# One scan over 128 partitions for both directions of an S5 layer, with ScalarE turning the states back, in a two-layer encoder trunk

## The chip, the core and the metric

The kernel runs on one core of a Trainium2 chip. The metric is the device time of one execution in microseconds (us), taken as the median of three runs. Five engines work side by side, each through its own queue and in program order: TensorE (PE in the rows, with its weight loads as PEld), VectorE (DVE), ScalarE (ACT), GpSimd (POOL) and SyncE (SP), which here issues the large loads. They wait for each other through semaphores.

## What is computed

The program is a trunk of two layers over 512 tokens of 1024 channels in float32. Layer 0 has a convolution and attention mixer, layer 1 a bidirectional state-space (S5) mixer; each is followed by a mixture of 16 experts. The change lies in the S5 mixer alone, cut here to its core:

```python
def s5_scan(u, ...):              # u: (B, S, 64 groups, 16); 64 complex states per group
    bu_re = jnp.einsum('bsgc,gpc->bsgp', u, bb_re)      # and bu_im
    # h_t = lambda * h_{t-1} + bu_t, complex, over the 512 tokens
    _, _, h_re, h_im = lax.associative_scan(combine, (a_re, a_im, bu_re, bu_im), axis=1)
    return (jnp.einsum('bsgp,gcp->bsgc', h_re, c_re)
            - jnp.einsum('bsgp,gcp->bsgc', h_im, c_im))

def s5_mixer(h, ...):
    y_f = s5_scan(u, ...)                                       # forward
    y_b = jnp.flip(s5_scan(jnp.flip(u, axis=1), ...), axis=1)   # backward, other parameters
    z = jax.nn.gelu((y_f + y_b).reshape(B, S, D) + d_skip * hf)
    val, gate = jnp.split(z @ w_glu, 2, axis=-1)
    return val * jax.nn.sigmoid(gate)
```

## The kernel before

The program runs four phases after each other: mixer 0, experts 0, mixer 1 (S5), experts 1. In mixer 1 the 512 tokens are cut into 64 chunks of 8 tokens. A state is carried from chunk to chunk by a scan, and what happens within a chunk is done by matmuls with tables that were prepared earlier. The 64 groups are worked in 8 **octets** of 8 groups. Partitions 0 to 63 hold the 64 states of the forward direction, partitions 64 to 127 those of the backward one.

Since the multiplier of a state is complex and DVE scans real numbers, the phase is taken out first by a table `E` and put back afterwards; the scan itself multiplies by the magnitude `rho` alone. For each octet there are five steps:

- `inputs(o)`: 32 matmuls on TensorE (64 rows of the trace, each matmul shown as two) take the tokens `U` into PSUM tiles (`mm` or `po`), 64 columns of the stationary `W` per direction, with `U` streamed.
- `turn_in(o)`: two DVE products (L1271, `t<-mm` or `t<-po`) and two POOL sums (L1290, L1291) give the scan's input `XP`; ACT lays out the multipliers `RT` with zeros between the groups (L1293 for the forward half, L1294 for the backward one).
- `scan(o)`: DVE scans real and imaginary part, each in two instructions: the forward half by L1304 and the backward half, with its operands read and written from the last chunk to the first, by L1306. Two DVE products with `E` (L1271, `t<-gr`) and two POOL sums (L1312, L1313) then give the states `Hs`.
- `outputs(o)`: 24 matmuls (48 rows) on TensorE, with `U` and `Hs` as stationary operands, into an `ac` tile, and a gelu on ACT (L1331) into `ZY`.
- `turn_z(q)`, for every second octet: eight transposes, and for each piece a copy on ACT (L1343) and a difference on DVE (L1344) into `zT`.

One loop staggers them. Its pass `o` issues, in this order: `inputs(o+1)`; `turn_u(o+2)`, which transposes the tokens of an octet (4 transposes, L202) and copies them to `U` (4 ACT copies, L206); `turn_in(o)`; `scan(o-1)`; in even passes from 4 on `turn_z`; `outputs(o-2)`. The order in each engine's queue is the order in which the code is written.

The tables come by DMA on SP's queue through eight buffers of 1 MB, in the order of use: `W` and `C` of an octet, and a block with `E` of one octet and `M` of the octet before (from `Ed` and `Ld`). A block is issued when a buffer's last reader is done. `self.stream.release` at the end of a pass frees the buffers.

The mixer ends with a dense stretch of matmuls with `w_glu` (L294), which needs `zT` of all octets. Then come a router and the second set of experts.

The table `E` is made in `s5_small` and `s5_phase` from a unit phase `PP`, whose imaginary part had a sign that differs between the two halves of the partitions.

Of the kernel before, what the change touches and what calls it, by code (L numbers as in the profile page):

```python
# [9 lines left out]
F32 = mybir.dt.float32  # L10
F32R = mybir.dt.float32r
I32 = mybir.dt.int32
AF = mybir.ActivationFunctionType
OP = mybir.AluOpType
# [10 lines left out]
H = 8  # L25
# [91 lines left out]
class Kern:  # L117
# [918 lines left out]
    def s5_small(self, q):  # L1036

        out = []
        v, dve = Later(self.nc.gpsimd, out), Later(self.nc.vector, out)
        mul, sub, add, ts, fma = self.arith(v)  # L1040

        PV, PC, PP, F, dg, rho = self.PV, self.PC, self.PP, self.F, self.dg, self.rho
        cnt = [0]

        def tl(n=None):
            cnt[0] += 1
            return q.tile([128, G], F32, name=n or f"t{cnt[0]}")
# [23 lines left out]
        d2 = self.d2  # L1071
        mul(dg, d2[:, 0], d2[:, 1])
        lr, li, ld = [self.lam[:, i] for i in range(3)]
        sgn = q.tile([128, 1], F32, name="sgn")
        v.memset(sgn[0:64], -1.0)
        v.memset(sgn[64:128], 1.0)
        den, d1 = tl(), tl()
        for o, x, y, op in ((den, lr, lr, OP.mult), (d1, li, li, OP.mult), (den, den, d1, OP.add)):
            dve.tensor_tensor(o, x, y, op=op)
# [5 lines left out]
        ang, n, r, z = tl(), tl(), tl(), tl()  # L1085
# [68 lines left out]
        U2 = q.tile([128, 2, 4, G], F32, name="U2")  # L1154
# [13 lines left out]
            cmul(U2, j, U2[:, :, j - 1], U2[:, :, j - 1])  # L1168
            unit(U2, j)
        v.tensor_copy(PP[:, 0, 0], U2[:, 0, 3])  # L1170
        v.tensor_scalar(PP[:, 1, 0], U2[:, 1, 3], sgn, None, op0=OP.mult)

        q3 = [L[:, i, 0:8] for i in range(2)]
        cr, ci = [U2[:, i, 3].unsqueeze(1).to_broadcast([128, 8, G]) for i in range(2)]
# [43 lines left out]
    def mixer1(self, front):  # L1218
        nc, tc, a = self.nc, self.tc, self.a
        v, pl = nc.vector, nc.gpsimd  # L1220
        with ExitStack() as c:
# [4 lines left out]
            U = up.tile([128, G, 64], F32, name="U")  # L1226
# [17 lines left out]
            st = {}  # L1244
            mp = c_s.enter_context(self.pool("m1t"))
# [20 lines left out]
            def tmp(i):  # L1266
                return mp.tile([128, 2, 8, 64], F32, name=f"t{i}", bufs=2)

            def both(t, x, e):

                v.tensor_tensor(t, x.unsqueeze(1).to_broadcast([128, 2, 8, 64]), e, op=OP.mult)  # L1271

            def inputs(o):
                z = st[o] = dict(W=self.stream.get().rearrange("p (r g m) -> p r g m", r=2, g=8))
                z["px"] = px = [self.mm(), self.po() if o % 2 else self.mm()]
                for ri in (1, 0):
                    for g in range(8):
                        for d in range(2):
                            nc.tensor.matmul(px[ri][d * 64:(d + 1) * 64, g * 64:(g + 1) * 64],
                                             z["W"][:, ri, g, d * 64:(d + 1) * 64], U[:, 8 * o + g],  # L1280
                                             start=True, stop=True)

            def turn_in(o):
                z = st[o]
                t = [tmp(i) for i in range(2)]
                px = [p.rearrange("p (g k) -> p g k", g=8) for p in z["px"]]
                for i in (1, 0):
                    both(t[i], px[i], z["E"])
                xq, rt = XP[o % 2], RT[o % 2]
                pl.tensor_tensor(xq[:, 0, :, 1:65], t[0][:, 0], t[1][:, 1], op=OP.subtract)  # L1290
                pl.tensor_tensor(xq[:, 1, :, 1:65], t[0][:, 1], t[1][:, 0], op=OP.add)  # L1291
                rv = self.rho[:, 8 * o:8 * o + 8].unsqueeze(2)
                nc.scalar.activation(rt[0:64, :, 1:64], rv[0:64].to_broadcast([64, 8, 63]), AF.Copy)  # L1293
                nc.scalar.activation(rt[64:128, :, 0:63], rv[64:128].to_broadcast([64, 8, 63]), AF.Copy)  # L1294

            def scan(o):
                z = st[o]
                gr = mp.tile([128, 2, 8, 66], F32, name="gr", bufs=2)
                gf = gr.rearrange("p r g k -> p r (g k)")
                xf, rf = [t[o % 2] for t in (XP, RT)]  # L1300
                xf, rf = xf.rearrange("p r g k -> p r (g k)"), rf.rearrange("p g k -> p (g k)")

                for ri in range(2):
                    v.tensor_tensor_scan(gf[0:64, ri], rf[0:64], xf[0:64, ri], initial=0.0,  # L1304
                                         op0=OP.mult, op1=OP.add)
                    v.tensor_tensor_scan(gf[64:128, ri, 525::-1], rf[64:128, 525::-1], xf[64:128, ri, 527:1:-1],  # L1306
                                         initial=0.0, op0=OP.mult, op1=OP.add)
                u = [tmp(i) for i in range(2)]
                for i in range(2):
                    both(u[i], gr[:, i, :, 0:64], z["E"])  # L1310
                z["H"] = Hs = mp.tile([128, 2, 8, 64], F32, name="Hs", bufs=2)
                pl.tensor_tensor(Hs[:, 0], u[0][:, 0], u[1][:, 1], op=OP.add)  # L1312
                pl.tensor_tensor(Hs[:, 1], u[1][:, 0], u[0][:, 1], op=OP.subtract)  # L1313

            def outputs(o):
                z = st[o]
# [34 lines left out]
            def accumulate(s, n, part):  # L1351
                if part != 1:
                    ps[s] = self.mm()[:, :256]
                ks = range(KC) if part is None else range(4) if part == 0 else range(4, 8)
                self.mm3(ps[s], lambda x, k: zT[x][:, k, s], lambda y, k: ws[n][y][:, k], ks, part)

            inputs(0)
            for o in range(8 + 3):
                if o + 1 < 8:
                    inputs(o + 1)  # L1360
                if o + 2 < 8:
                    turn_u(o + 2)
                if 2 <= o < 10:
                    t = self.stream.get()
                    st[o - 2]["C"] = t.rearrange("p (r g m) -> p r g m", r=2, g=8)
                if o < 9:
                    t = self.stream.get()
                    if o < 8:
                        st[o]["E"] = t[:, 1024:].rearrange("p (r g k) -> p r g k", r=2, g=8)
                    if o >= 1:  # L1370
                        st[o - 1]["M"] = t[:, :1024].rearrange("p (t q b c) -> p b q t c", t=8, q=4, b=2)
                if o < 8:
                    turn_in(o)
                if 1 <= o < 9:
                    scan(o - 1)
                if o >= 4 and o % 2 == 0:
                    turn_z((o - 4) // 2)
                if o == 8:

                    for s in range(3):  # L1380
                        accumulate(s, 0, 0)
                if 2 <= o < 10:
                    outputs(o - 2)
                if o == 6:
                    self.next_split(self.bigp, 1, False, 0)
                if o == 7:
                    ws.append(self.next_split(self.bigp, 1, False, 1))

                self.stream.release((o == 0) + (1 <= o < 10) + (o + 1 < 8) + (2 <= o < 10))
# [513 lines left out]
```

## Time and profile before

| | us |
|---|---|
| median of 3 runs (1560.76 to 1565.56) | 1564.18 |
| profiled execution, its own time | 1567.34 |
| its span in the trace | 1565.5 |
| PE busy | 1420.1 |
| DVE busy | 712.9 |
| POOL busy | 495.2 |
| ACT busy | 380.3 |

The span runs from the first instruction to the last; the profiled execution's own time has 1.8 us more, which lie around it. Busy times are sums over the whole span. TensorE is busy for 91% of it, but that is a mean over phases with different limits, so a stage is read by itself. The loop over octets described above lies at about 867 to 980 us of the span.

### The profile page before, as it was taken

The page shows a single profiled execution, that of the slowest core. Times are in us where ns is not written, and L with a number is a line of the kernel's source. Part 1 is how long each engine was busy: PE and PEld are TensorE (multiplying, and loading weights), DVE is VectorE, ACT ScalarE, POOL GpSimd, SP SyncE. Part 2 cuts the span into 40 slices and gives each one's busy share as a digit, 9 for nine tenths or more (in the row PEclk, how much of TensorE's full clock was granted, in tenths as well). Part 3 has the DMA queues.
Part 4 walks back from the last instruction along what each step waited for, and adds up shares of the span by engine and source line. Part 5 has one row for each costly group of instructions (what it writes and reads, how often), then busy time and mean ns, then how long its engine had stood idle before and what let it go on. Part 6 is the DMA issues. An engine that isn't in the chain of part 4 may idle for free. (4 is left out here: it accounts for less than half of the span.)

```text
span 1565.5 us, 22806 instructions
## 1 busy us (share of the span) xinstructions
PE 1420.1 (91%) x9196; PEld 836.1 (53%) x9196; DVE 712.9 (46%) x1148; ACT 380.3 (24%) x826; POOL 495.2 (32%) x795
## 2 busy tenths in 40 slices
PE   7899999899999897979899765999899999999998
PEld 6698667854434342424246655998433333333335
DVE  3788555511176657566322897335122221221122
ACT  5165664301111111111113422446011111111111
POOL 6998342000066377662500654422000000000000
PEclk8899999999999999999999877999999999999999
DMA  4231217469799999999999976622699999999998
GB/s 140 85 132 55 71 35 288 188 249 420 302 349 408 414 407 413 415 405 419 418 419 406 284 235 220 255 105 81 260 420 419 420 420 419 420 418 421 419 419 323
DMA packets 78569, 485.17 MB, mean 310 GB/s; under 512 B 10112, under 2 KB 12928, under 8 KB 24576
## 3 DMA queue, kind: packets, MB, share of 16 engines
q1 hardware_dynamic: 66896, 457.86, 73.3%
q0 software_dynamic: 5504, 16.19, 2.8%
q10 hardware_dynamic: 6064, 9.66, 1.6%
q8 instruction: 72, 1.18, 0.3%
q14 instruction: 33, 0.27, 0.0%
HBM read 459.63 MB, written 24.05 MB: 309 GB/s over the span
## 5 line engine op out<-in xcount | busy, mean ns | idle before, releaser
L858 PE MATMUL mm<-w,xi 128*64 128x512 f32 x2048 | 473.1, 606 | 38.3 <-DMA w<-in_w_e_up 29.9
L858 PEld LDWEIGHTS mm<-w,xi 128*64 128x64 f32 x2048 | 139.7, 138 | 322.8 <-issue 246.3
L910 PE MATMUL po<-w,h 128*64 128x512 f32 x896 | 206.4, 601 | 0.0
L910 PEld LDWEIGHTS po<-w,h 128*64 128x64 f32 x896 | 59.3, 137 | 107.0 <-issue 105.3
L800 DVE TENSOR_TENSOR R<-R,ac 128x512 f32<-128x512 f32 x112 | 71.8, 682 | 93.3 <-PE ac L798 93.3
L883 DVE TENSOR_TENSOR h<-h,mm 128x256 f32<-128x256 f32 x60 | 22.5, 416 | 154.5 <-PE mm L858 154.5
L360 DVE SCALAR_TENSOR_TENSOR ac<-hp,vec,ac 128x512 f32<-128x512 f32 x116 | 87.5, 754 | 3.0
L284 POOL TENSOR_TENSOR wlo<-w,whi 128x1024 fp32r<-128x1024 f32 x30 | 71.7, 2409 | 33.4 <-ACT whi L283 33.3
L294 PE MATMUL mm<-whi,xT 128*128 128x256 f32 x384 | 72.0, 287 | 2.7 <-DVE ast L474 2.5
L882 ACT ACTIVATE h<-mm 128x256 f32<-128x256 f32 x60 | 19.8, 381 | 218.1 <-PE mm L858 218.1
L727 DVE TENSOR_TENSOR xi<-tr,vec 128x512 f32<-128x512 f32 x32 | 22.1, 691 | 99.2 <-PE tr L737 58.5
L208 DVE COPY OE<-po 64x512 f32<-64x512 f32 x28 | 19.4, 694 | 104.9 <-ACT OE L206 104.8
L206 ACT ACTIVATE OE<-po 64x512 f32<-64x512 f32 x28 | 16.5, 590 | 195.4 <-PE po L910 195.4
L737 PEld LDWEIGHTS tr<-Dm,hn 128*128 128x128 f32 x512 | 59.7, 197 | 6.8 <-ACT h L882 6.0
L294 PEld LDWEIGHTS mm<-whi,xT 128*128 128x128 f32 x384 | 61.0, 193 | 3.9 <-DVE ast L474 3.4
L1624 POOL DMA_DIRECT2D gn<-in_mix_norm_odd x8 | 4.7, 593 | 181.2 <-PE mm L858 137.1
L1325 PE MATMUL ac<-w,Hs 128*64 128x128 f32 x256 | 33.2, 396 | 31.5 <-POOL Hs L1312 26.1
L737 PE MATMUL tr<-Dm,hn 128*128 128x128 f32 x512 | 61.2, 282 | 0.0
L294 PE MATMUL mm<-wlo,xT 128*128 128x256 f32 x192 | 54.8, 285 | 0.0
L1741 POOL DMA_DIRECT2D Ld<-Lt x32 | 18.4, 582 | 108.7 <-DVE Lt L1019 101.5
L722 DVE TENSOR_TENSOR Dm<-slot,io 128x512 f32<-128x512 f32 (+1 forms) x16 | 11.1, 696 | 86.4 <-PE tr L202 86.3
L797 PE MATMUL ac<-OH,DT 128*128 128x512 f32 x112 | 50.3, 449 | 0.0
(376 smaller groups left out, 2562.6 us busy)
## 6 DMA issues: line engine op xcount, KB each, us to landing
w<-in_w_e_gate SPq DMA_DIRECT2D x128, 1024.0 KB, 16.7
w<-in_w_e_up SPq DMA_DIRECT2D x128, 1024.0 KB, 16.1
w<-in_w_e_down SPq DMA_DIRECT2D x112, 1024.0 KB, 15.6
w<-in_w_e_tail SPq DMA_DIRECT2D x16, 1024.0 KB, 19.0
w<-in_w_in SPq DMA_DIRECT2D x9, 1024.0 KB, 4.7
Wd<-Wt ACTq DMA_DIRECT2D x32, 256.0 KB, 10.6
Cd<-CE POOLq DMA_DIRECT2D x16, 512.0 KB, 13.2
w<-Wd SPq DMA_DIRECT2D x8, 1024.0 KB, 12.5
```

Source lines behind the costliest of these rows:

```text
L284: (nc.vector if fast else nc.gpsimd).tensor_tensor(lo[:, o], w[:, o], hi[:, o].bitcast(F32), op=OP.subtract)
L294: self.nc.tensor.matmul(out, st(i, k), mv(j, k), start=n == 0, stop=n == 3 * KC - 1)
L360: v.scalar_tensor_tensor(cv[:, ch] if j == CW - 1 else acc, hp[:, ch, j:j + S], cw[:, ch, j:j + 1], acc, op0=OP.mult, op1=OP.add)
L727: v.tensor_tensor(P[j]["xi"][:, 4 * hf:4 * hf + 4], p.rearrange("p (k c) -> p k c", k=4), g[:, 4 * hf:4 * hf + 4].unsqueeze(2).to_broadcas ...
L737: nc.tensor.matmul(p[:, k * 128:(k + 1) * 128], hn[:, s, kk * 128:(kk + 1) * 128], Dm[:, s].rearrange("p e c -> p (e c)"), start=s == 0, s ...
L797: nc.tensor.matmul(p, DT, P[j]["hi"], start=True, stop=False)
L800: v.tensor_tensor(rv, rv, p, op=OP.add)
L858: nc.tensor.matmul(p[hf * 64:(hf + 1) * 64], xi[:, k, r:r + CAP], w[:, o:o + 512], start=k == 0, stop=k == KC - 1)
L882: nc.scalar.activation(h[:, o], pg[:, o], AF.Silu)
L883: v.tensor_tensor(h[:, o], h[:, o], pu[:, o], op=OP.mult)
L910: nc.tensor.matmul(po[dh * 64:(dh + 1) * 64], hT[:, c4 * 128 + hf * 64:c4 * 128 + hf * 64 + 64], w[:, o:o + 512], start=i == 0, stop=i == 7)
L1325: nc.tensor.matmul(ov, lh, rh, start=n == 0, stop=n == 2)
```

## The change

Before, the backward half was scanned from the last chunk to the first by instructions of its own. Now its chunks are laid out from the last to the first already when they are made: the matmuls of `inputs` stream `U` with the 64 chunks reversed for direction 1. The scan then runs over all 128 partitions in one direction, and `E` turns the same way in both halves, so the sign goes. The states of the backward half come out in reversed order. A new step `ordered(o)` on ACT copies `Hs` to a new tile `Ho`, the upper half with its chunks reversed, and `outputs` reads `Ho`. It is called in pass `o+2`, behind `turn_u` and ahead of `turn_in`. `Hs` has one buffer now and `Ho` two. The four scan instructions of an octet become two, and the two layouts of `RT` become one.

```diff
@@ s5_small
-        sgn = q.tile([128, 1], F32, name="sgn")
-        v.memset(sgn[0:64], -1.0)
-        v.memset(sgn[64:128], 1.0)
...
-        v.tensor_scalar(PP[:, 1, 0], U2[:, 1, 3], sgn, None, op0=OP.mult)
+        ts(PP[:, 1, 0], U2[:, 1, 3], -1.0)
@@ mixer1, inputs
                             nc.tensor.matmul(px[ri][d * 64:(d + 1) * 64, g * 64:(g + 1) * 64],
-                                             z["W"][:, ri, g, d * 64:(d + 1) * 64], U[:, 8 * o + g],
+                                             z["W"][:, ri, g, d * 64:(d + 1) * 64],
+                                             U[:, 8 * o + g, ::-1] if d else U[:, 8 * o + g],
                                              start=True, stop=True)
@@ mixer1, turn_in
-                nc.scalar.activation(rt[0:64, :, 1:64], rv[0:64].to_broadcast([64, 8, 63]), AF.Copy)
-                nc.scalar.activation(rt[64:128, :, 0:63], rv[64:128].to_broadcast([64, 8, 63]), AF.Copy)
+                nc.scalar.activation(rt[:, :, 1:64], rv.to_broadcast([128, 8, 63]), AF.Copy)
@@ mixer1, scan
                 for ri in range(2):
-                    v.tensor_tensor_scan(gf[0:64, ri], rf[0:64], xf[0:64, ri], initial=0.0,
-                                         op0=OP.mult, op1=OP.add)
-                    v.tensor_tensor_scan(gf[64:128, ri, 525::-1], rf[64:128, 525::-1], xf[64:128, ri, 527:1:-1],
-                                         initial=0.0, op0=OP.mult, op1=OP.add)
+                    v.tensor_tensor_scan(gf[:, ri], rf, xf[:, ri], initial=0.0, op0=OP.mult, op1=OP.add)
...
-                z["H"] = Hs = mp.tile([128, 2, 8, 64], F32, name="Hs", bufs=2)
+                z["H"] = Hs = mp.tile([128, 2, 8, 64], F32, name="Hs")
...
+            def ordered(o):
+
+                Hs = st[o]["H"]
+                st[o]["H"] = Ho = mp.tile([128, 2, 8, 64], F32, name="Ho", bufs=2)
+                nc.scalar.activation(Ho[0:64], Hs[0:64], AF.Copy)
+                nc.scalar.activation(Ho[64:128], Hs[64:128, :, :, ::-1], AF.Copy)
@@ mixer1, the loop
+                if 2 <= o < 10:
+                    ordered(o - 2)
                 if o < 8:
                     turn_in(o)
```

The first place is ACT's queue in pass 3, from the copies of `U` of octet 5 to the gelu of octet 1 (`-` is the row of before, `+` the row of now; a number behind a name is a buffer's).

```order
 L206 ACTIVATE U<-tr 64x4x64 x4
-L1293 ACTIVATE RT_6640<-rho 64x8x63
-L1294 ACTIVATE RT_6640<-rho 64x8x63
-L1331 ACTIVATE ZY<-ac 128x4x8x16
+L1313 ACTIVATE Ho<-Hs 64x1024
+L1314 ACTIVATE Ho<-Hs 64x1024
+L1291 ACTIVATE RT_6637<-rho 128x8x63
+L1332 ACTIVATE ZY<-ac 128x4x8x16
```

The two copies to `Ho` stand behind the four copies to `U` and ahead of everything else of the pass; one row to `RT` stands where two stood.

The second place is DVE's queue around the scan of octet 1, first as it was, from the second product of `turn_in(2)` to the products with `E`.

```order
L1271 TENSOR_TENSOR t_6886<-mm,w 128x1024
L1304 SCALAR_TENSOR_TENSOR gr<-RT_6640,XP_6637 64x528
L1306 SCALAR_TENSOR_TENSOR gr<-RT_6640,XP_6637 64x526
L1304 SCALAR_TENSOR_TENSOR gr<-RT_6640,XP_6637 64x528
L1306 SCALAR_TENSOR_TENSOR gr<-RT_6640,XP_6637 64x526
L1271 TENSOR_TENSOR t_6899<-gr,w 128x1024
L1271 TENSOR_TENSOR t_6900<-gr,w 128x1024
```

The same place of the changed program, up to the first product of `turn_in(3)`:

```order
L1268 TENSOR_TENSOR t_6882<-mm,w 128x1024
L1301 SCALAR_TENSOR_TENSOR gr<-RT_6637,XP_6634 128x528 x2
L1268 TENSOR_TENSOR t_6892<-gr,w 128x1024
L1268 TENSOR_TENSOR t_6893<-gr,w 128x1024
L1268 TENSOR_TENSOR t_6980<-po,w 128x1024
```

The four scans of an octet are two, over twice the partitions, and the products with `E` follow them directly. The orders of TensorE and SP are as they were, but for the tile that `outputs` reads.

## Rows read from the trace of the kernel before

**Rows 1.** Busy time by stretch: each engine's us and instructions, granted clock, DMA share, GB/s.
```profile
880.00:900.00 20.00, 13.12 (x178) 12.16 (x180) 19.81 (x15) 6.86 (x12) 13.55 (x8) 0.75 0.89 270
...
1080.00:1100.00 20.00, 17.03 (x127) 16.61 (x128) 16.30 (x33) 10.51 (x18) 10.20 (x8) 0.84 0.22 91
...
1120.00:1140.00 20.00, 18.93 (x92) 6.46 (x90) 2.73 (x5) 3.30 (x8) 0.00 (x0) 1.00 1.01 419
```

**Rows 2.** Timeline of DVE and POOL, octet 1: start, duration, instruction, idle before.
```profile
883.62 1.57 DVE L1304 TENSOR_TENSOR_SCAN gr<-RT,XP 64x528 f32<-64x528 f32 x1
885.23 2.14 DVE L1306 TENSOR_TENSOR_SCAN gr<-RT,XP 64x526 f32<-64x526 f32 x1
...
886.22 2.21 POOL L1291 TENSOR_TENSOR XP<-t,t 128x512 f32<-128x512 f32 x1
...
887.40 2.14 DVE L1304 TENSOR_TENSOR_SCAN gr<-RT,XP 64x528 f32<-64x528 f32 x1
...
889.57 1.25 DVE L1306 TENSOR_TENSOR_SCAN gr<-RT,XP 64x526 f32<-64x526 f32 x1
890.85 2.36 DVE L1271 TENSOR_TENSOR t<-gr,w 128x1024 f32<-128x1024 f32 x2
...
895.40 1.50 DVE L1304 TENSOR_TENSOR_SCAN gr<-RT,XP 64x528 f32<-64x528 f32 x1
```

**Rows 3.** Two lines by themselves: count, ns of the shortest, median and longest.
```profile
L1562 DVE TENSOR_TENSOR_SCAN cu<-wk x2: 1211/1212/1212, 311.5 to 1095.5; 16x512 f32<-16x512 f32 x2
...
L283 ACT ACTIVATE whi<-w x32: 1039/1047/1076, 15.1 to 1046.3; 128x1024 fp32r<-128x1024 f32 x32
```

**Rows 4.** Timeline of PE and ACT, outputs(0) to outputs(1).
```profile
884.14 0.69 PE L1325 MATMUL ac<-w,Hs 128*64 128x128 f32 x4 [0.79 <-POOL Hs L1313]
...
888.46 2.80 PE L1279 MATMUL mm<-U,w 128*64 128x64 f32 x64
891.19 0.66 PE L202 MATMUL tr<-ident,xs 128*128 128x128 f32 x4
891.88 1.56 ACT L206 ACTIVATE U<-tr 64x256 f32<-64x256 f32 x4 [2.57 <-PE tr L202]
...
894.61 0.44 PE L1325 MATMUL ac<-w,Hs 128*64 128x128 f32 x4 [2.39 <-POOL Hs L1312]
...
896.11 0.39 PE L1325 MATMUL ac<-w,U 128*64 128x128 f32 x4
...
896.76 0.44 PE L1325 MATMUL ac<-w,U 128*64 128x128 f32 x4
```

**Rows 5.** Busy time by stretch, columns as in rows 1.
```profile
884.00:890.00 6.00, 5.86 (x70) 5.86 (x72) 5.91 (x4) 0.60 (x1) 4.43 (x3) 0.50 1.00 283
891.00:896.00 5.00, 1.82 (x25) 1.10 (x21) 5.00 (x5) 2.76 (x6) 2.71 (x3) 1.00 0.76 243
...
868.00:940.00 72.00, 46.72 (x730) 41.84 (x725) 69.33 (x52) 23.26 (x48) 41.47 (x26) 0.81 0.83 253
```

**Rows 6.** Timeline, all engines, places from the loop's first table load to its end.
```profile
867.95 0.32 SPq L211 DMA_DIRECT2D w<-Wd  x1
...
924.28 1.10 PE L1279 MATMUL po<-U,w 128*64 128x64 f32 x32
...
926.36 0.32 SPq L244 DMA_DIRECT2D w<-Ed  x1
...
927.56 0.40 SPq L211 DMA_DIRECT2D w<-Cd  x1
...
957.70 2.05 POOL L1312 TENSOR_TENSOR Hs<-t,t 128x512 f32<-128x512 f32 x1 [4.94 <-DVE t L1271]
...
959.72 2.21 POOL L1313 TENSOR_TENSOR Hs<-t,t 128x512 f32<-128x512 f32 x1
...
975.83 0.60 ACT L1331 ACTIVATE ZY<-ac 128x512 f32<-128x512 f32 x1 [4.68 <-PE ac L1325]
...
979.71 0.42 DVE L1344 TENSOR_TENSOR zT<-tr,zT 128x256 fp32r<-128x256 f32 x1 [0.46 <-ACT zT L1343]
```

**Rows 7.** DMA issues from 926.3 to 926.7 us: size, us from issue to landing.
```profile
w<-Ed SPq DMA_DIRECT2D x1, 512.0 KB, 8.0
```

## The prediction

> **What bounds the kernel now.** I read the busy time by stretch first, since the change touches one stage only. In the S5 loop DVE is busy for 19.81 of 20 us, TensorE for 13.12 at a mean granted clock of 0.75 [rows 1]: DVE sets the pace. The timeline of DVE shows why. The scan of octet 1 starts at 883.62 and that of octet 2 at 895.40, 11.8 us later, and 7.20 of these are the four scan instructions, from 883.62 to 890.82 [rows 2]. The same timeline shows what the others wait for: TensorE stands at the first matmul with `Hs` of octet 1 until POOL is done (2.39 us idle), and POOL waits 4.94 us for DVE's products [rows 4, 6].
>
> The stage ends with the last difference into `zT`, at 979.71 + 0.42 = 980.13 [rows 6]. What follows needs it and shifts with it: a dense stretch of matmuls, the router, the experts. The experts' weights are the last limit of the kernel (1.01 of DMA time, 419 GB/s from 1120 on), but while the router works the DMA engines are busy for 0.22 only [rows 1]: their loads wait for buffers that the experts free, so the stream starts earlier if the experts do.
>
> **What the change does, part by part.**
>
> *The scans.* Two of four go. Elements run along the columns: a scan over 16 partitions and 512 columns takes 1.21 us [rows 3], one over 64 partitions and 526 columns with nothing beside it 1.25 [rows 2]. So I price one over 128 partitions at 1.25 too. The bounds are 1.25 and twice that; four times the partitions changed nothing between the two rows, so I take the lower end. Beside POOL's sums for `XP` a scan takes 2.14 instead of 1.25, and the sum 2.21 [rows 2]. The first two scans of the octet end at 887.37, so the scan part falls from 7.20 to 3.75, by 3.45 us. POOL's second sum, 886.22 to 888.43, now lies beside the first product with `E` instead of the third scan. No row shows that product beside a sum; it costs between 0 and what a scan pays, 2.14 - 1.25 = 0.9. I take 0.9, since the product reads two tiles of SBUF as the scan does. DVE's octet falls from 11.8 to 8.3 to 9.2 us.
>
> The Trainium skill speaks against the change here ("SBUF — State Buffer", section "SBUF: two separate sides"): a DVE instruction with two SBUF inputs and a GpSimd instruction that reads SBUF exclude each other for a whole instruction. The slowed scans agree with it. By it the octet would be 9.2 us, without it 8.3.
>
> *The copies to `Ho`.* ACT copies 128x1024 in 1.047 us [rows 3]; the two halves have 1024 columns each, so 2.1 us for both. The second reads backwards: between nothing and double (1.05 more). DVE's backward scan cost no more than a forward one (1.25 against 1.21), so I take nothing. The one layout of `RT` that goes lies beside other work.
>
> *A new wait.* The copies stand behind the four copies to `U` in ACT's queue, and these need transposes that TensorE issues behind `inputs`. TensorE's `outputs` now waits for ACT, and what is queued behind it (the next `inputs`) waits too. That closes a loop through TensorE and ACT, once per pass while there are copies to `U`:
> - `inputs`: 64 rows take 2.73 at the lower clock (888.46 to 891.19), 1.97 at the higher one (from 924.28 to just before the issue of `Ed` that it releases at 926.36, less 0.1) [rows 4, 6];
> - transposes and copies to `U`: 891.19 to 893.44, 2.25 [rows 4];
> - copies to `Ho`: 2.1, and hand-overs of 0.15;
> - the 44 rows of `outputs` that stand behind `Ho`: at 1.2 GHz 40 rows take 4.32 (884.14 to 888.46, granted clock 0.50), so 4.75; at 2.4 GHz 12 rows take 0.65 (896.11 to 896.76), so 2.4 [rows 4, 5].
>
> The sum is 8.9 at the higher clock and 12.0 at the lower one. TensorE has no more than a few matmuls with `U` for some 4 us of each pass while ACT copies. Behind the wait for `Hs` of octet 0 the rows show the clock at 0.50 from 884 to 890, with TensorE busy, and at 1.00 from 891 to 896 [rows 5]. I take a point two thirds towards the lower clock: 10.9 for the loop and 3.9 for `outputs`. The loop, not DVE's 9.2, then sets the pace for octets 1 to 3.
>
> *Reversed `U`.* 32 of the 64 rows of `inputs` stream backwards. No row shows that on TensorE: between nothing and double, which is 1.0 us per octet at the higher clock. I take nothing, as for DVE.
>
> *The sign* in `s5_small` removes two memsets 500 us earlier; nothing waits for them.
>
> *The sum.* `outputs(0)` ends as before, at 888.5: 3.45 less for scans against 2.2 for the copies and the 1.2 us by which the first half of `Hs` used to come earlier. Three loops of 10.9 end `outputs(3)` at 921.2, against 924.28 before [rows 6]: only 3 us are won there. Then the chain is: `inputs(7)` 2.5, 923.7; its end releases the buffer for `E` of octet 7, as before (926.36), which lands 8.0 later [rows 7], 931.8; products of `turn_in(7)` 2.4, 934.2; scan of octet 6 3.75, 937.9; products 2.36 + 0.9, 941.2; `Hs` beside the next scan 4.2 (957.70 to 961.93), 945.5; `Ho` 2.3, 947.8; `outputs(6)` 3.9, 951.7; gelu 0.7, 952.4; `Ho` of octet 7 2.2, 954.6; `outputs(7)` 3.9, 958.5; from its gelu to the last `zT` 4.3 as before (975.83 to 980.13) and 0.1, 962.9. The stage ends 980.1 - 962.9 = 17.2 us earlier. The profiled execution would take 1567.3 - 17.2 = 1550.1. It lies 3.2 above the median of the runs, so for the median I forecast 1564.2 - 17.2 = **1547**.
>
> **The rivals.**
>
> *TensorE stays at the lower clock through the loop.* Three loops of 12.0 end `outputs(3)` 3.3 later than in the sum, and the two last `outputs` cost 0.85 more each. The gain is 12.2: 1552. For it speak the pauses in every pass, against it that the rows show 1.00 within some 7 us of work.
>
> The Trainium skill ("TensorE: Matmul & The Clock Gate", section "HAM oscillation") tells of a kernel that fell back to the lower clock in each tile because it waited in each; that would be this case.
>
> *A backward read costs double*, on ACT or TensorE. The first adds 1.05 to three loops and to two copies of the last chain, 5; the second about 1 to `inputs` 4 to 7, 4. The gain is 12 to 13, and 8 with the lower clock: 1552 to 1556.
>
> *The table loads become the bound.* From 868 to 940 the DMA engines are busy for 0.83 of 72 us, 59.8 [rows 5], and between the issues at 867.95 and 927.56 [rows 6] lie 16 blocks: 3.74 us each. An octet needs three, 11.2 us. If that set the pace, 0.6 per octet would be won, 5 in all, less the last octet's copies: a gain of 3, 1561. Against it: eight blocks are loaded ahead, and `E` of octet 7, the 15th, could land by 868 + 15 x 3.74 = 924, before the 931.8 of the sum.
>
> *The gain is lost downstream* in the weights' stream: 1564. The idle DMA engines ahead of it speak against that.
>
> *Slower: streaming `U` backwards is far dearer.* Every us on `inputs` lies about six times on the path (octet 0 and 1 at the start, 4 to 6 in the loop, 7 in the last chain). The 17.2 are gone at 2.9 us per octet, where the 32 reversed rows cost four times their 1.0; at five times they give 4 x 6 - 17.2 = 7 more, 1571. No row speaks for so much.
>
> **How the numbers follow.** Chances: the sum as forecast 0.53, the lower clock 0.16, a backward read that costs double 0.12, loads as the bound 0.06, lost downstream 0.05, slower 0.08. The forecast's own range goes from a high clock with DVE as the bound (9.2 per octet; the last chain 3 shorter, the loops 5 to 6: 1540) to 1552. With the third case it is 1541 to 1558, which leaves out the last three. A difference of 0.3%, 4.7 us, is about what can be told from no change here. Faster by more than that: the first three cases, 0.81. Within it: loads and downstream, 0.11. Slower: 0.08.
>
> **What the changed profile would show.** Two scans over 128x528 per octet of some 1.6 to 2.2 us each; DVE with pauses in the loop, where it had none; TensorE waiting for ACT's `Ho` and no longer for POOL's `Hs`; gelus of octets 0 to 3 hardly earlier, the last ones by 15 us and more; the last `zT` near 963. I would be wrong if a scan took 2.5 alone, if `inputs` took clearly more than 2.0 at the higher clock, if `turn_in` waited for `E` in most octets, or if the last `zT` came earlier and the end did not.

## The result and the profile after

| | before | after |
|---|---|---|
| median of the runs, us | 1564.85 (1560.76 to 1565.56, 4 runs) | 1549.79 (1547.17 to 1550.43, 4 runs) |
| profiled execution: its own time | 1567.34 | 1547.17 |
| the stage, from a load of `W` to the end of the last `zT` | 112.18 | 97.41 |
| VectorE busy | 712.9 | 692.2 |
| ScalarE busy | 380.3 | 392.2 |

The ratio of the times is 0.9912, with a 95% interval from 0.9894 to 0.9931: 15 us faster, where 17 were forecast (1547).

The stage is the measure used below. It runs from the issue of the load of `W` for octet 4 (867.95 before [rows 6], 863.14 after) to the end of the last difference into `zT` (980.13 before, 960.55 after). The trace of after is 4.8 us ahead at its start already, so the positions of the two traces can't be compared directly. The kernel after was run once more later, as `e12_after_again`: there the stage took 99.37 us. So a stage from one execution is good to about 2 us, and the change is worth 12.8 to 14.8 us in it. From the last `zT` to the end the span has 585.40 us before and 584.83 after: nothing is lost downstream.

Busy time by stretch in the kernel after, with columns as in rows 1:

```profile
863.00:913.00 50.00, 33.81 (x598) 30.78 (x596) 47.09 (x36) 25.77 (x46) 34.89 (x22) 0.85 0.97 292
875.00:895.00 20.00, 12.83 (x176) 12.35 (x178) 19.25 (x14) 9.95 (x15) 15.22 (x10) 0.74 0.96 273
```

VectorE is busy for 19.25 of 20 us, as it was before (19.81 [rows 1]). It does more octets in them, and it is still the engine with hardly a pause, where pauses were forecast. The last but one number, the share of the DMA engines, has risen to 0.96 and 0.97 from 0.89.

The timeline of VectorE and GpSimd around octets 1 and 2, which answers to rows 2:

```profile
873.84 2.34 DVE L1268 TENSOR_TENSOR t<-mm,w 128x1024 f32<-128x1024 f32 x2
...
876.11 3.74 DVE L1301 TENSOR_TENSOR_SCAN gr<-RT,XP 128x528 f32<-128x528 f32 x2
...
876.52 2.22 POOL L1288 TENSOR_TENSOR XP<-t,t 128x512 f32<-128x512 f32 x1
...
878.70 2.22 POOL L1289 TENSOR_TENSOR XP<-t,t 128x512 f32<-128x512 f32 x1
...
879.78 3.36 DVE L1268 TENSOR_TENSOR t<-gr,w 128x1024 f32<-128x1024 f32 x2
883.06 1.21 DVE L1268 TENSOR_TENSOR t<-po,w 128x1024 f32<-128x1024 f32 x1
```

The two scans take 3.74 us where the four took 7.20. GpSimd's second sum, from 878.70 to 880.92, now lies over the first product with `E`, and the two products take 3.36 where they took 2.36. From the first product of `turn_in(2)` to that of `turn_in(3)` it is 883.06 - 873.84 = 9.2 us, against 11.8.

The groups of VectorE's instructions in the stage of after (count, busy time, mean ns, idle time before them and what ended it):

```profile
L1301 DVE TENSOR_TENSOR_SCAN gr<-RT,XP 128x528 f32<-128x528 f32 x16 | 29.3, 1870 | 1.1 <-ACT RT L1291 1.1
L1268 DVE TENSOR_TENSOR t<-gr,w 128x1024 f32<-128x1024 f32 x16 | 28.0, 1789 | 0.0
L1268 DVE TENSOR_TENSOR t<-mm,w 128x1024 f32<-128x1024 f32 x12 | 14.3, 1215 | 5.2 <-DMA w<-Ed 4.1 <-PE mm L1276 1.2
```

The same groups before:

```profile
L1306 DVE TENSOR_TENSOR_SCAN gr<-RT,XP 64x526 f32<-64x526 f32 x16 | 29.2, 1825 | 0.4
L1304 DVE TENSOR_TENSOR_SCAN gr<-RT,XP 64x528 f32<-64x528 f32 x16 | 29.1, 1818 | 1.3 <-ACT RT L1293 1.1
L1271 DVE TENSOR_TENSOR t<-gr,w 128x1024 f32<-128x1024 f32 x16 | 18.9, 1222 | 0.2
L1271 DVE TENSOR_TENSOR t<-mm,w 128x1024 f32<-128x1024 f32 x12 | 14.3, 1216 | 1.2 <-PE mm L1279 1.2
```

The scans were busy for 29.1 + 29.2 = 58.3 us and the products with `gr` for 18.9. So 29.0 were saved and 9.1 given back, 2.5 per octet net. Of the 9.1, about 6 are the 1.0 in each of octets 1 to 6. Another 3.2 lie in octet 7 alone, whose products take 5.54 us beside a GpSimd instruction that prepares the next stage (a block of `w_glu`):

```profile
941.68 5.54 DVE L1268 TENSOR_TENSOR t<-gr,w 128x1024 f32<-128x1024 f32 x2
...
942.79 3.35 POOL L284 TENSOR_TENSOR whl<-w,whl 128x1024 fp32r<-128x1024 f32 x1
```

The end of the line for `t<-mm` in after is new: VectorE waits 4.1 us for `E`, where it did not wait for it before.

The end of the stage, in the timeline of after, from the issue of the `E` of octet 7:

```profile
913.98 0.32 SPq L244 DMA_DIRECT2D w<-Ed  x1
...
914.57 1.52 PE L1276 MATMUL po<-U,w 128*64 128x64 f32 x32
...
917.00 2.36 DVE L1268 TENSOR_TENSOR t<-mm,w 128x1024 f32<-128x1024 f32 x2 [3.30 <-DMA w<-Ed]
...
928.00 0.43 DVE L1345 TENSOR_TENSOR zT<-tr,zT 128x256 fp32r<-128x256 f32 x1 [0.47 <-ACT zT L1344]
...
928.55 1.22 DVE L1268 TENSOR_TENSOR t<-po,w 128x1024 f32<-128x1024 f32 x1
...
947.39 1.27 POOL L1306 TENSOR_TENSOR Hs<-t,t 128x512 f32<-128x512 f32 x1 [1.25 <-DVE t L1268]
...
949.11 0.58 ACT L1332 ACTIVATE ZY<-ac 128x512 f32<-128x512 f32 x1
...
949.93 1.06 ACT L1313 ACTIVATE Ho<-Hs 64x1024 f32<-64x1024 f32 x1 [0.24 <-POOL Hs L1307]
951.00 1.05 ACT L1314 ACTIVATE Ho<-Hs 64x1024 f32<-64x1024 f32 x1
952.10 0.66 PE L1326 MATMUL ac<-w,Ho 128*64 128x128 f32 x8 [2.74 <-ACT Ho L1314]
...
956.25 0.60 ACT L1332 ACTIVATE ZY<-ac 128x512 f32<-128x512 f32 x1 [4.21 <-PE ac L1326]
...
960.13 0.42 DVE L1345 TENSOR_TENSOR zT<-tr,zT 128x256 fp32r<-128x256 f32 x1 [0.46 <-ACT zT L1344]
```

The issue at 913.98 and its time to landing:

```profile
w<-Ed SPq DMA_DIRECT2D x1, 512.0 KB, 14.5
```

`turn_in(6)` stands 3.30 us for its `E`. The `E` of octet 7 lands at 913.98 + 14.5, about 928.5, just as VectorE comes free (928.00 + 0.43), and `turn_in(7)` starts at 928.55. So octet 7 hardly waits. But its `E` was issued before `turn_in(6)` began, so it would have held `turn_in(7)` until then even if octet 6 had had its own `E` early. From 928.55 the stage takes 32.0 us, against 35.4 before, and the two copies to `Ho` with `outputs(7)` are the piece from 949.93 to 956.25. Two paths end almost together ahead of it: the gelu of octet 6 at 949.69, and GpSimd's last sum for octet 7, for which ScalarE waits 0.24 us more.

### The profile page after: what moved, and what is told of

The parts are those of the page before. It is cut to its first block, busy times and chain, and to the rows that moved or that the text cites. A ratio compares the mean times of both kernels' runs of the same rounds, so it can differ in the third digit from the quotient of the medians.

```text
span 1545.4 us, 22796 instructions
## 1 busy us (share of the span) xinstructions
PE 1409.9 (91%) x9196; PEld 828.6 (54%) x9196; DVE 692.2 (45%) x1132; ACT 392.2 (25%) x834; POOL 499.3 (32%) x793
## 5 line engine op out<-in xcount | busy, mean ns | idle before, releaser
L858 PE MATMUL mm<-w,xi 128*64 128x512 f32 x2048 | 473.7, 606 | 38.6 <-DMA w<-in_w_e_up 30.9
L1326 PE MATMUL ac<-w,Ho 128*64 128x128 f32 x256 | 28.3, 361 | 27.4 <-ACT Ho L1314 27.4
L206 ACT ACTIVATE h<-tr 128x256 f32<-128x256 f32 (+1 forms) x58 | 22.7, 391 | 106.8 <-PE tr L202 106.8
```

The source lines that it names most:

```text
L206: self.nc.scalar.activation(out, in_, AF.Copy)
L858: nc.tensor.matmul(p[hf * 64:(hf + 1) * 64], xi[:, k, r:r + CAP], w[:, o:o + 512], start=k == 0, stop=k == KC - 1)
L1326: nc.tensor.matmul(ov, lh, rh, start=n == 0, stop=n == 2)
```

## The experiments

Each edit is to the kernel after. The table has what the timelines of the one profiled execution of each kernel give: the passes (from the first product of one `turn_in` to that of the next, octets 1 to 7), VectorE's wait for `E` in all of them, the time from the `W` load to `turn_in(7)`, from there to the last `zT`, the sum of these two, which is the stage, and the median of the runs.

| kernel | passes, us | wait for E | to turn_in(7) | from it | stage | median, us |
|---|---|---|---|---|---|---|
| before | 12.06 11.77 11.71 14.25 11.45 14.22 | 0 | 76.8 | 35.4 | 112.2 | 1565 |
| after | 9.35 9.21 10.08 11.59 12.27 11.55 | 4.1 | 65.4 | 32.0 | 97.4 | 1549.8 |
| e12, after again | 9.36 9.21 11.58 11.89 11.63 11.38 | 5.3 | 66.4 | 33.0 | 99.4 | 1552.5 |
| e5, scans cut | 12.05 11.76 11.79 14.25 11.43 14.24 | 0 | 76.9 | 36.9 | 113.8 | 1569.3 |
| e2, no copies | 9.36 9.23 9.38 11.49 11.87 11.33 | 3.1 | 64.0 | 29.5 | 93.5 | 1548.2 |
| e1, copies first | 9.36 9.21 9.26 11.72 11.11 11.37 | 2.1 | 63.4 | 32.1 | 95.5 | 1550.9 |
| e3, warm | 9.35 9.35 11.06 12.19 12.03 11.47 | 5.6 | 66.8 | 30.6 | 97.4 | 1550.1 |
| e4, plain M | 9.36 9.21 9.26 11.73 8.89 11.72 | 0 | 61.5 | 33.1 | 94.6 | 1544.8 |
| e6, copies cut | 9.35 9.22 10.17 11.38 10.84 11.34 | 2.7 | 63.7 | 32.5 | 96.2 | 1548.2 |
| e8, first and warm last | 9.36 9.22 9.25 11.72 9.16 12.72 | 1.4 | 62.8 | 30.9 | 93.7 | 1548.6 |
| e9, three edits | 9.36 9.23 9.23 11.73 8.89 11.68 | 0 | 61.5 | 32.6 | 94.0 | 1550.3 |
| e7, pad | 9.35 12.07 12.33 12.74 11.35 12.03 | 10.4 | 71.2 | 32.9 | 104.1 | 1550.6 |
| e10, two Ld | 9.36 14.19 14.54 13.97 13.92 13.50 | 20.0 | 80.8 | 30.4 | 111.2 | 1567.7 |

A stage stands for one execution only. The profiled one was the shortest of its kernel's runs in after, e3, e6 and e8, and the longest in before, e7 and e12, so stages a few us apart are no ranking. Two things are read from the table before any single run. Where `E` is in time, the first passes are 9.2 to 9.4 us whatever is done to ScalarE and TensorE. And the time to `turn_in(7)` is 61.5 us plus the wait for `E`, within 0.7, in every kernel of the table with whole scans: up to there the stage is VectorE's work and this wait, and nothing else adds to it.

**e5: cut the scans.** This undoes the merged scans alone.

```diff
-    v.tensor_tensor_scan(gf[:, ri], rf, xf[:, ri], ...)
+    for h in (slice(0, 64), slice(64, 128)):
+        v.tensor_tensor_scan(gf[h, ri], rf[h], xf[h, ri], ...)
```

> The kernel after, with each scan over 128 partitions cut into two scans over 64 partitions in the same direction; the reversed chunks, the copies into Ho and the placing stay. Theory (the merged scans alone are the gain; a half scan lasts as long as a whole one): the scans of an octet go from 3.7 back to about 7.3 us, a VectorE pass from 9.4 to about 13, and the stage, which is 97.4 us from the load of the fourth W to the last zT, becomes 115 to 122, that is longer than the 112.2 of the kernel before, since the copies and the slower products by E stay: about 1565 to 1574. Rival (the gain comes from shorter waits elsewhere, such as reading U backward instead of two scan directions): 1550 to 1556.

Measured: 1569.27 us, ratio to before 1.0029 (1.0012 to 1.0047); stage 113.8. VectorE's groups in its stage:

```profile
L1302 DVE TENSOR_TENSOR_SCAN gr<-RT,XP 64x528 f32<-64x528 f32 x32 | 58.4, 1824 | 1.5 <-ACT RT L1291 1.1
L1268 DVE TENSOR_TENSOR t<-gr,w 128x1024 f32<-128x1024 f32 x16 | 18.9, 1222 | 0.3
```

The whole gain is the scans': cut, they take 58.4 us again, every pass is that of before to 0.1 us, and what remains of the change, the copies among it, makes the kernel 0.3% slower than before. The stage is shorter than expected, because the products are at 18.9 again: with 7 us of scans the sum of GpSimd no longer reaches them. So their 9.1 us are a price of the shorter scans and not of the new layout.

**e2: leave the copies out.**

```diff
-    z["H"] = Hs = mp.tile([128, 2, 8, 64], F32, name="Hs")
+    z["H"] = Hs = mp.tile([128, 2, 8, 64], F32, name="Hs", bufs=2)
...
-    if 2 <= o < 10:
-        ordered(o - 2)
```

> The turning back is left out: the outputs read Hs as it is, so the backward direction's chunks stand in reversed order in what is computed. Theory one (ScalarE's copies set the pace): 4 to 7 us off, up to 3 of it in the first four octets, the rest the two copies (2.1 us each) of the last two octets that lie in the last chain. Rival (the table loads set the pace): about 4 us off, all of it in the last chain after octet 7's states, with a longer wait for E at turn_in of octets 5 to 7. Third: the copies are hidden throughout, and less than 1 us comes off.

Measured: 1548.2 us (0.9898 of before, 0.9868 to 0.9928); stage 93.5, 3.9 less. The first products of `turn_in` in its timeline:

```profile
877.65 2.34 DVE L1268 TENSOR_TENSOR t<-mm,w 128x1024 f32<-128x1024 f32 x2
886.88 1.21 DVE L1268 TENSOR_TENSOR t<-po,w 128x1024 f32<-128x1024 f32 x1
...
896.25 2.36 DVE L1268 TENSOR_TENSOR t<-mm,w 128x1024 f32<-128x1024 f32 x2 [0.16 <-DMA w<-Ed]
907.75 1.23 DVE L1268 TENSOR_TENSOR t<-po,w 128x1024 f32<-128x1024 f32 x1
...
919.62 2.35 DVE L1268 TENSOR_TENSOR t<-mm,w 128x1024 f32<-128x1024 f32 x2 [2.90 <-DMA w<-Ed]
```

The passes stay: 9.23 from 877.65 to 886.88, as in after. Of the 3.9 us, 2.5 lie behind `turn_in(7)`, about the 2.1 of the last octet's two copies, and 1.0 is less waiting for `E`. So the rival's 4 us came, but not the longer wait for `E` that went with it. The copies do not set the pace of the loop, though TensorE waits 27.4 us for `Ho` in the profile of after; it has that time to spare.

**e1: the copies first in each pass.**

```diff
     for o in range(8 + 3):
+        if 2 <= o < 10:
+            ordered(o - 2)
         if o + 1 < 8:
             inputs(o + 1)
...
-        if 2 <= o < 10:
-            ordered(o - 2)
         if o < 8:
             turn_in(o)
```

> The copies into Ho are issued at the top of the pass, ahead of the copies of U and of the inputs' matmuls, so that ScalarE does them first. Theory one (the chain of ScalarE's Ho copies and TensorE's outputs and inputs sets the pace of the first four octets, where a pass takes 10.35 us on average and TensorE waits up to 9.8 us for Ho): a pass falls to about 9, bounded by VectorE's 9.2 to 9.7, and the stage ends 3 to 4 us earlier. Rival (the table loads are nearly the bound: their DMA share is .93 to 1.01 there, and octet 6's E lands 13.2 us after its issue): the passes shorten, but turn_in of octets 5 to 7 waits longer for E, and the stage ends 0 to 1 us earlier.

Measured: 1550.9 us (0.9903, 0.9874 to 0.9933); stage 95.5. The first passes are 9.2 as in after, so theory one's mechanism is not there; what differs is the wait for `E`, 2.1 instead of 4.1, where the rival expected a longer one. Between two executions of after it differs by 1.2, so this says little more than that the place of the copies hardly matters.

**e3: keep TensorE busy ahead of the outputs.**

```diff
     py = self.ac()
+    for _ in range(10):
+        nc.tensor.matmul(py[:, :128], self.ident, self.ident, start=True, stop=True)
```

> Ten matmuls of 128 columns that nobody reads are put ahead of each octet's output matmuls, where TensorE waits for Ho. Theory one (the low granted clock, .74 to .85 in the stage, lengthens the outputs, which sit in the loop and in the last chain): outputs fall from 4.1 to 5.1 us to about 2.6 to 3, the last chain by about 3, and the stage ends 3 to 5 us earlier. Rival (VectorE or the loads set the pace, or the added matmuls only stand in the way): no change, or up to 2 us later.

Measured: 1550.1 us (0.9899, 0.9868 to 0.9930); stage 97.4, the same. The last octet:

```profile
952.82 0.66 PE L1328 MATMUL ac<-w,Ho 128*64 128x128 f32 x8 [1.64 <-ACT Ho L1314]
...
955.49 0.60 ACT L1334 ACTIVATE ZY<-ac 128x512 f32<-128x512 f32 x1 [2.72 <-PE ac L1328]
```

Here `outputs(7)` needs 2.67 us (952.82 to 955.49), against 4.15 in after (952.10 to 956.25). The granted clock of the two pieces, first in after and then in e3 (the number ahead of the share of the DMA engines):

```profile
952.00:956.30 4.30, 4.12 (x44) 3.71 (x44) 0.00 (x0) 0.09 (x2) 0.00 (x0) 0.62 0.84 351
```

```profile
952.80:955.50 2.70, 2.62 (x44) 2.38 (x44) 0.00 (x0) 0.01 (x1) 0.00 (x0) 1.00 1.00 413
```

So the lower clock costs 1.5 us in the last chain. In the loop the faster outputs bring nothing, as VectorE sets the pace.

**e4: read M from another place.**

```diff
-    L = self.Ld[o - 1]
-    nc.sync.dma_start(t[:, :1024], bass.AP(tensor=L.tensor, offset=L.offset,
-                                           ap=[[128, 8], [15 * 128, 16], [1, 1024]]))
+    L = self.Cd[o - 1].rearrange("p r g m -> p (r g m)")
+    nc.sync.dma_start(t[:, :1024], L[:, :1024])
```

> The M half of each E and M block is read from a contiguous piece of the C tables of the same size, where it is read in an overlapping pattern of 512-byte pieces now: the bytes loaded are the same in number, the values of M are not those the reference needs. Theory of the loads (a transfer in many small pieces makes the loads a bound): the landing of E falls from 10 to 14 us to 8 or less, the 3.3 us wait at turn_in of octet 6 is gone, and the stage ends about 3 us earlier. Rival (the loads are limited by bytes and not by pieces): landings stay within 1 us, no change. Second rival (the loads don't bind at all): the landings fall and the time stays.

The expectation is wrong on one point: the pieces have 1024 elements, 4096 bytes, in both patterns; only where they start differs. Measured: 1544.8 us (0.9868, 0.9846 to 0.9891), the fastest of all; stage 94.6. `E` loads issued from 868 to 915 us, size and median landing time, first in after, then in e4:

```profile
w<-Ed SPq DMA_DIRECT2D x5, 512.0 KB, 12.4
```

```profile
w<-Ed SPq DMA_DIRECT2D x5, 512.0 KB, 3.7
```

VectorE no longer waits for `E`, and `turn_in(7)` comes at 61.5. So the loads of `M` are what makes `E` late, though `E` has the same bytes and place in both and is issued within 0.7 us of the same time after the load of `W` that begins the stage.

**e7: other distances between the rows of Ld.**

```diff
-    self.Ld = dr.tile([8, 16, 15, 4, 32], F32, name="Ld")
+    self.Ld = dr.tile([8, 16, 16, 4, 32], F32, name="Ld")
...
-    ap=[[128, 8], [15 * 128, 16], [1, 1024]]
+    ap=[[128, 8], [16 * 128, 16], [1, 1024]]
```

> The rows of the Ld table in DRAM lie 8192 bytes apart, where they lie 7680 apart now; the loads of M read the same number of bytes in the same pieces of 4096 bytes, still overlapping. Theory one (the loads of M are slow because of where the pieces start): the landing of E falls from 12.4 us toward the 3.7 us with M from a contiguous place, and the stage falls by 2 to 3 us from 97.4. Theory two (they are slow because every byte of a small area is read up to eight times, wherever the rows start): no change, the landing of E stays within 2 us of 12.4.

Measured: 1550.6 us over nine runs (0.9927, 0.9906 to 0.9947), as after. Its profiled execution was the longest of the nine, 1559.07, and its stage of 104.1 with it; `E` landed in 15.9 us there and VectorE waited 10.4 us for it. (2.78 of the 10.4 are put down to GpSimd by the profile; but that `E` landed at 890.91 and the product started at 891.04.) Nothing speaks for theory one. Theory two is not shown by it either: the landing is not within 2 us of 12.4.

**e10: two copies of Ld, two half loads.**

```diff
-    L = self.Ld[o - 1]
-    nc.sync.dma_start(t[:, :1024], bass.AP(..., ap=[[128, 8], [15 * 128, 16], [1, 1024]]))
+    for h in range(2):
+        L = self.Ld[o - 1, h]
+        nc.sync.dma_start(t[h * 64:(h + 1) * 64, :1024], bass.AP(..., ap=[[128, 4], [15 * 128, 16], [1, 1024]]))
...
-    nc.gpsimd.dma_start(k.Ld[o, :, :, gq], ...)
+    for h in range(2):
+        nc.gpsimd.dma_start(k.Ld[o, h, :, :, gq], ...)
```

> The kernel after, with two copies of the Ld table in DRAM, written by two sets of stores, and each half of M's partitions read from its own copy, so that each byte is read half as often. Theory (many reads of one small area are what makes the loads of M slow): the landing of E falls from 12.4 us by a third or more, and the stage by 1 to 3 us from 97.4; the 32 more stores cost GpSimd some 18 us of issuing where it has idle time, 0 to 2 us of the span. Rival (reading twice from a table costs the same wherever the copies lie): the landing stays, no change or up to 2 us more.

Measured: 1567.7 us (1.0021 of before, 1.0008 to 1.0033): the gain is gone. VectorE waits 20.0 us for `E`. Both theories missed this. The run changed two things at once, as its queue has five loads to an octet instead of four, and now waits for earlier loads to land:

```profile
SPq L244 <- DMA w<-Ld: 10.2, 3, 4.2
...
SPq L249 <- DMA w<-Cd: 9.7, 5, 2.5
```

With the smaller groups it waits 34.6 us for landings in the stage, where the queue of after waits for none. How much of the loss is this and how much the slower load itself is not separated. What tells is the DMA share late in the stage, where the queue issues nothing for some us, or only `M`, and what is left to finish is `M` and what stands behind it. First after, then e10, then e4, columns as in rows 1:

```profile
922.00:926.00 4.00, 0.00 (x0) 0.00 (x0) 4.00 (x4) 0.00 (x0) 1.76 (x1) 0.97 0.52 179
```

```profile
943.00:949.00 6.00, 0.44 (x4) 0.23 (x4) 5.30 (x6) 0.87 (x3) 3.61 (x3) 0.75 0.26 89
```

```profile
922.00:923.00 1.00, 0.00 (x0) 0.00 (x0) 1.00 (x2) 0.00 (x0) 0.00 (x0) 1.00 0.04 16
```

The share is a mean over 16 engines. It stays at 0.52 for 4 us in after and at 0.26 for 6 us in e10: as with half of the engines at work (8.3 of 16), and with a quarter of them (4.2). The rate per engine at work is the same, 179 / 8.3 and 89 / 4.2, some 21 GB/s. The trace of before has the same level late in its stage, in the same order of loads:

```profile
933.00:936.00 3.00, 2.66 (x26) 2.66 (x28) 2.97 (x2) 0.00 (x0) 3.00 (x3) 0.50 0.54 194
```

In e4 the loads end together, and nothing is left. The slowest dimension of the load's source has 8 entries in after, 4 in e10 and 128 in e4. That fits a load that is spread over as many engines as this dimension has entries, up to 16. The Trainium skill states just that ("DMA: Bandwidth & Descriptors", section "Rules for kernel authors": an outermost dimension of fewer than 16 confines a transfer to at most that many engines), and the shares here agree with it. The account that follows is argued and not shown: the half of the engines that carries `M` falls behind, and `E`, spread over all 16, is there only when the slowest has done its part. A kernel that keeps the values of `M` and loads them in eight pieces of 16 partitions would test it; it was not run.

**e6: cut the copies into four.**

```diff
-    nc.scalar.activation(Ho[0:64], Hs[0:64], AF.Copy)
-    nc.scalar.activation(Ho[64:128], Hs[64:128, :, :, ::-1], AF.Copy)
+    for ri in range(2):
+        nc.scalar.activation(Ho[0:64, ri], Hs[0:64, ri], AF.Copy)
+        nc.scalar.activation(Ho[64:128, ri], Hs[64:128, ri, :, ::-1], AF.Copy)
```

> The two copies into Ho are cut into four, real part first, so that the first two can run beside GpSimd's second sum. Theory (the copies stand in the chain from GpSimd's second sum to TensorE's outputs, 2.1 us of it): about 1 us comes off the last chain, and up to 1 us in each early pass where VectorE and the loads let it through; the stage is 1 to 2.5 us shorter than 97.4. Rival (the loads and VectorE set the pace everywhere but in the last chain, and each copy has a fixed part): 0 to 0.7 us.

Measured: 1548.2 us (0.9907, 0.9880 to 0.9934); stage 96.2; the wait for `E`, 1.4 shorter, covers the difference. The last octet:

```profile
946.10 0.58 ACT L1333 ACTIVATE ZY<-ac 128x512 f32<-128x512 f32 x1
...
946.70 0.63 ACT L1314 ACTIVATE Ho<-Hs 64x512 f32<-64x512 f32 x1
...
948.63 0.63 ACT L1315 ACTIVATE Ho<-Hs 64x512 f32<-64x512 f32 x1
```

The cut gains nothing in the last chain: ScalarE is at the gelu of octet 6 while GpSimd makes the second sum, and four copies take 2.5 us instead of 2.1. The rival holds.

**e8 and e9: edits together.** e8 has e1's order and 24 matmuls ahead of `outputs(7)` alone; e9 has e6's cut as well.

```diff
     py = self.ac()
+    for _ in range(24 if o == 7 else 0):
+        nc.tensor.matmul(py[:, :128], self.ident, self.ident, start=True, stop=True)
```

> Two edits together: the copies into Ho first in each pass (alone 1.9 us off the stage), and 24 matmuls that nobody reads ahead of the last octet's outputs alone, where TensorE waits for Ho (with 10 ahead of every octet's outputs the last chain was 1.5 us shorter, and the passes before it as much longer). If the two are independent the stage falls from 97.4 to about 94 us. Rival: the added matmuls end after Ho is there and delay the outputs (24 of them at the low clock are 2.6 us), so that the stage is as in the run with the copies first, 95.5, or longer.

> Copies into Ho first in each pass, cut into four (real part first), and 24 matmuls that nobody reads ahead of the last octet's outputs alone: the first and third had a stage of 93.7 us together, the cut alone took 1.2 off 97.4. If they add up the stage is 92.5 to 93 us, some 4.5 us under the kernel after. Rival: the cut gains nothing where the copies already come first, and the stage stays at 93.7.

Measured: e8 1548.6 us (0.9904, 0.9871 to 0.9937), stage 93.7; e9 1550.3 (0.9917, 0.9903 to 0.9932), stage 94.0. Both stages are near what was expected, but not by the reasons given. In e8, of the 3.7 us by which the stage is shorter than in after, 2.7 are a shorter wait for `E`. The added matmuls take over 5 us, twice the 2.6 of the expectation, so they end 1.2 us after `Ho` is there (949.03 against 947.86):

```profile
943.73 5.30 PE L1320 MATMUL ac<-ident 128*128 128x128 f32 x46
...
946.81 1.05 ACT L1314 ACTIVATE Ho<-Hs 64x1024 f32<-64x1024 f32 x1
```

In e9 VectorE does not wait for `E` at all, and the last chain gains nothing (32.6):

```profile
952.26 5.62 PE L1321 MATMUL ac<-ident 128*128 128x128 f32 x48
...
955.71 0.63 ACT L1315 ACTIVATE Ho<-Hs 64x512 f32<-64x512 f32 x1
957.81 0.44 PE L1329 MATMUL ac<-w,U 128*64 128x128 f32 x4
```

`Ho` is there at 956.3; the added matmuls last until 957.9. What the outputs gain at the higher clock is lost by starting 1.5 us late. Against after, which ran beside e9 as e12 (1552.5; 0.9924, 0.9910 to 0.9937), the intervals overlap: no version that keeps the computation whole is shown to beat the kernel after.

**e12: the kernel after once more.**

> The kernel after as it is, once more beside these, since single executions differ by some us before the stage begins: a stage within 1 us of 97.4, and 1547 to 1552 us.

Measured: 1552.5 us (0.9924, 0.9910 to 0.9937), stage 99.4: 2 us from the first execution, where 1 was expected, and the median half a us above the range; 1.2 of the 2 are the wait for `E`.

**e11**, the edits of e9 and e10 together:

> The three edits to copies and matmuls and the two copies of Ld together. If both gain: a stage of 90.5 to 92 us. If the two copies of Ld give nothing: 92.5 to 93.7 as in the run with the three edits.

Measured: 1563.6 us (1.0000, 0.9985 to 1.0015), stage 109.1. That is 15 us longer than in e9, from which it differs by the two copies of `Ld` alone; they cost here what they cost in e10.

## Why the prediction was right, and where its steps were not

- **Scans.** Priced at 1.25 us alone and 3.75 for the pair; the shortest took 1.245, and the pairs 3.42 to 3.78 up to octet 4. Twice the partitions cost nothing. e5 shows that the whole gain is here.
- **The first product beside GpSimd's sum.** Taken as 0.9, measured 1.0 (3.36 against 2.36). That the products of octet 7 would stand beside GpSimd's work for the next stage (5.54) was not in the sum. By the rule that the two exclude each other, from the Trainium skill ("SBUF — State Buffer", section "SBUF: two separate sides"), VectorE's octet was to be 9.2; the trace agrees, with passes of 9.2 where `E` is in time.
- **Copies and reversed reads.** The plain copy took 1.056 us at the median and the reversed one 1.053. A row of `inputs` has a median of 222 ns before and after. Both were taken as free, and are; the rivals of a dear backward read fall.
- **The pace of the loop: wrong.** "The loop, not DVE's 9.2, then sets the pace for octets 1 to 3" fails. With the loop cut open (e2), or its copies moved (e1), the passes stay at 9.2 to 9.4. VectorE sets the pace; a pass with `turn_z` is 11.7 and one with a late `E` longer. So VectorE has hardly a pause, where the prediction expected pauses. The loop through TensorE and ScalarE was priced with the low clock and the copies behind those to `U`, 10.9; the starts of `inputs` are 10.35 apart in the mean (883.51 to 914.57 in three passes), but because TensorE waits there for VectorE's states, by way of GpSimd and ScalarE. That the forecast of 10.9 came near is chance. One of its terms is also misread: the 2.73 us of `inputs` from 888.46 to 891.19 span both levels of the clock, as the granted clock (the number ahead of the share of the DMA engines) shows in before:

```profile
888.00:890.00 2.00, 2.00 (x38) 2.00 (x36) 1.97 (x2) 0.60 (x1) 0.43 (x1) 0.50 0.99 352
890.00:892.00 2.00, 2.00 (x48) 1.74 (x44) 1.97 (x3) 0.12 (x1) 0.00 (x0) 0.96 0.83 336
```

- **`E` of octet 7 as the step that sets `turn_in(7)`: right place, wrong terms.** It was to be issued at the end of `inputs(7)`, 55.8 us after the load of `W` (923.7 - 867.95), and to land 8.0 later. It was issued ahead of `inputs(7)`, at 50.8 (913.98 - 863.14), and landed 14.5 later, just as VectorE came free. The wait that shows is that of octet 6, 3.30 us, which the sum did not have. The rival of the loads was put aside because eight blocks are loaded ahead at 3.74 us each. That mean hides that, while a load of `M` is left to finish, half of the engines are idle (0.54 in before, 0.52 in after). Late `E` costs 4.1 us of the stage (e4 takes them away), not the 14 of the rival.
- **The sum.** The errors offset each other: VectorE's faster passes put `turn_in(7)` at 61.5 us, had `E` been in time, and the forecast had 63.9 (931.8 - 867.95); it came at 65.4. That an `E` issued 4.9 us earlier than forecast, and 6.5 us longer on its way, lands so near the forecast is luck. From there 31.1 were forecast and 32.0 measured. The path that was added up there, through `Hs`, `Ho`, `outputs` and gelu of octet 6, ended 0.24 us before the copies of octet 7 started; the other one, through octet 7's own scan and products, ended last. Together the stage won 14.8 us of the 17.2.
- **The low clock.** It is real (0.74 to 0.85 by stretch) and cost the last outputs 1.5 us (e3), but in the loop nothing.
- **Downstream.** 585.40 and 584.83 us: the gain arrived whole.

## What to carry to other kernels

When an engine that sets the pace is relieved, look next at the loads that it used to cover: at 11.8 us a pass a late table was free, at 9.2 it cost 4.1 us beside the 14.8 that the change won. A long wait in the profile (TensorE's 27.4 us for `Ho`) is no proof of a bound; take its cause away and see whether the pace changes. And an instruction made shorter can uncover another that now collides with what used to run beside the first: close to a third of the scans' gain (9.1 of 29.0 us) went to the products that way.

## What the runs showed of the hardware that was not expected

- The load of `M`, where it is left to finish, keeps 0.52 of the DMA engines busy, and 0.26 with a slowest dimension of half the size, at 179 and 89 GB/s; loads of `E` with 128 rows land in 12.4 us beside it, and in 3.7 where `M` too is read with 128 rows.
- Issuing the load of `M` takes the queue 0.60 us with a slowest dimension of 8, and 0.32 to 0.39 with 128 (e4).
- In e10, with five loads to an octet, the queue waits 34.6 us for earlier loads to land; in after, with four, not at all.
- With the code ahead of the stage all but unchanged, the stage began between 861.69 and 867.90 us in nine executions (after twice, e1 to e6 and e8), and at 870.97 in e9. Single times therefore tell less of a stage than its own length does; what makes the difference was not looked into.
